# Key transposes and the spread of 1/rms as one group behind the first gate pass of a hybrid decoder layer

## The chip, the cores and the metric

The kernel runs on one core of a Trainium2 chip. The metric is the time on the device in microseconds (us). Its engines are called PE (TensorE; PEld is its weight load), DVE (VectorE), ACT (ScalarE), POOL (GpSimd) and SP (SyncE, which here issues the loads). Each engine works through its own row of instructions in order; where one needs the result of another engine, it waits for a semaphore, and everything behind it on that engine waits with it.

## What is computed

One decoder layer on 256 tokens of width 2048, all in float32. The part around the change is the input projection and what is made of its keys:

```python
h = rmsnorm(x, norm_mix_pre[l])
proj = h @ w_in[l]
xr, yr, q, k, v, g_rnn, g_attn = jnp.split(proj, IN_OFFSETS, axis=-1)
...
q = rope(q.reshape(B, S, N_Q_HEADS, HEAD_DIM), positions)
k = rope(k.reshape(B, S, N_KV_HEADS, HEAD_DIM), positions)
v = v.reshape(B, S, N_KV_HEADS, HEAD_DIM)
y_att = sliding_window_sink_attention(q, k, v, attn_sinks[l])
mix = jax.nn.sigmoid(g_rnn) * (y_rnn @ w_rnn_proj[l]) + jax.nn.sigmoid(g_attn) * (y_att @ w_attn_proj[l])
x = x + rmsnorm(mix @ w_out[l], norm_mix_post[l])
h = rmsnorm(x, norm_mlp_pre[l])
u = jnp.square(jax.nn.relu(h @ w_mlp_up[l]))
x = x + rmsnorm(u @ w_mlp_down[l], norm_mlp_post[l])
```

There are 32 query heads and 4 key and value heads of width 64. `rmsnorm` scales each token by 1/rms; `rope` rotates pairs of columns by angles that depend on the token's position.

## The kernel before

**Products in two parts.** A float32 weight is split into a high part (rounded, `whi`, made by ACT, L117) and a low part (the rest, `wlo`, made by DVE, L123). The transposed activations `hT` are split alike, and a product is three matmuls: high by high, low by high, high by low.

**Weights in half chunks.** `Stream` (from L64) brings the weights in half chunks of 128 x 1024 values, 512 KB each, numbered in the order of use. Raw ones land in four `wraw` buffers (more at the start), high and low parts live in six buffers each (`WHALF`). Before a half chunk is used, `ahead` (L149) sees to it that the parts of six half chunks are written down and that loads run four further. The high part of half chunk n needs the buffer of n - 6, which PE gives back when it is done with that one. A load needs a raw buffer, which DVE's low part gives back.

**Order of work.** After the normalisation and the keys' and values' product (half chunks 0 to 7, banks `kv0` and `kv1`, one for each block of 128 tokens) come four pairs of passes by `b_pass512` (L324): the gate `ga0` (half chunks 8 to 15), the queries `q0` (16 to 23), then `ga1`, `q1` and so on. A half chunk is twelve matmuls of 512 columns. These matmuls and the transposes are pinned in PE's row in the order in which the program is written (`fix`, `ordered`); the rows of ACT and DVE are set by the scheduler, which places instructions by its own rules.

**Side work.** Attention is a generator in the list `waiting`. `pump` (L257) advances it to its next `yield`. In the gate and query passes it is called after each half chunk (`often=True`). The generator begins with `keys_values` (L619). For each block it has ACT scale the values out of the bank, lets DVE rotate the keys (`rope`, L600, which needs sine and cosine of the angles, L567 to L586, times 1/rms of the token) into `k2`, yields, has PE transpose the four groups of `k2` into a bank `pk` and ACT copy them to `kT`, and yields again. At its end `spread_r` (L592) has DVE make two diagonal tiles `dg`, PE multiply them by ones into the bank `pr`, and ACT copy this to `r_all`: 1/rms of every token in every row.

So with one `pump` for each half chunk the first block's rotation is written behind half chunk 8, its transposes behind 9, the second block's transposes behind 11, and the spread behind 12. `kT` is first read by the scores of attention in `ga1`, `r_all` by the recurrent branch (L825) after all eight passes. The banks `pk` and `pr` come from a pool of four, `psm`, which also holds `kv0` and `kv1`; `k2`, the rotation's tiles `ra` and `rb`, and `dg` come from eight rooms `t2`.

## Time and profile before

| | us |
|---|---|
| time, median of 3 runs (1512.39 to 1516.35) | 1514.12 |
| time of the profiled execution | 1514.38 |
| its span, from the first to the last instruction | 1512.6 |
| PE busy | 1490.0 |
| DVE busy | 1126.3 |
| ACT busy | 808.9 |
| HBM traffic, mean over the span | 195 GB/s |

Times in the trace are microseconds from the start of the span. In rows of instructions the first number is the start, the second the length, then follow engine, line, operation and tiles (buffer numbers left out). Matmuls overlap, so the step from one start to the next says what one costs. In a row of waits stand the total, how many, and the longest. The granted clock of PE is given as a share of its full speed.

### The profile page before, as it was taken

Reading aid. Unit: us, or ns where it says so; the run is one execution under the profiler, and the core shown is the slowest. Engines: PE = TensorE matmul, PEld = TensorE weight load, DVE = VectorE, ACT = ScalarE, POOL = GpSimd, SP = SyncE. Lnnn points to the kernel's source line nnn. Section 1 sums busy time; section 2 is a strip of 40 time slices with the busy share of each in tenths; the row PEclk is TensorE's granted clock in tenths of the full one; section 3 lists DMA queues with packets and bytes.
Section 4 is the critical chain, followed back from the end, with each engine's and each line's share of the span. In section 5 each row is a group of like instructions: output and inputs, shape, how many; then the busy total and the mean of one; then the engine's idle time right before and its main releaser. Section 6 shows DMA issues by size and latency. Waiting matters only on the chain.

```text
span 1512.6 us, 19987 instructions
## 1 busy us (share of the span) xinstructions
PE 1490.0 (99%) x7586; PEld 1259.5 (83%) x7586; DVE 1126.3 (74%) x1417; ACT 808.9 (53%) x1110; POOL 1.7 (0%) x9
## 2 busy tenths in 40 slices
PE   9899999999999999999999999999999999999997
PEld 7688778878888888888889888888887888888886
DVE  7557668857758877545667876689987766789898
ACT  6436545747556767444446545455554544555453
POOL 0000000000000000000000000000000000000000
PEclk9899999999999999999999999999999999999999
DMA  7454445365655565656755665655666656578573
GB/s 288 143 189 162 139 157 180 124 202 161 215 177 181 168 224 186 216 191 213 270 192 169 205 208 182 193 195 197 223 216 223 201 180 202 175 252 277 167 252 137
DMA packets 83184, 296.19 MB, mean 196 GB/s; under 512 B 9745, under 2 KB 10001, under 8 KB 82577
## 3 DMA queue, kind: packets, MB, share of 16 engines
q1 hardware_dynamic: 80064, 289.67, 58.3%
q10 hardware_dynamic: 3024, 5.25, 0.9%
q8 instruction: 59, 0.97, 0.3%
q14 instruction: 37, 0.30, 0.1%
HBM read 288.60 MB, written 6.29 MB: 195 GB/s over the span
## 4 chain that ended last, share of the span: by engine, by line
PE 85%; DVE 9%; DMA 4%; ACT 1%; issue 1%; DVEq 0%; SPq 0%; ACTq 0%
PE ps L200 25%; PE ga L200 6%; PE ps L282 6%; PE q L200 6%; DMA wraw<-in_w_dn 4%; PE dQ L200 4%; DVE wlo L123 3%; DVE t L61 3%; PE ps L290 3%; PE s L200 3%; PE dP L200 2%; PE pa L314 2%; PE gr L318 2%; PE pa L318 2%; PE pr L318 2%; PE gr L316 2%
## 5 line engine op out<-in xcount | busy, mean ns | idle before, releaser
L123 DVE TENSOR_TENSOR wlo<-wraw,whi 128x1024 fp32r<-128x1024 f32 x520 | 621.2, 1220 | 242.3 <-ACT whi L117 215.3
L117 ACT CAST whi<-wraw 128x1024 fp32r<-128x1024 f32 x520 | 531.8, 1050 | 432.5 <-DVE wraw L61 77.3
L200 PE MATMUL ps<-h2T,whi 128*128 128x512 f32 x976 | 227.1, 390 | 0.0
L200 PEld LDWEIGHTS ps<-h2T,whi 128*128 128x128 f32 x976 | 181.3, 188 | 36.4
L200 PEld LDWEIGHTS ps<-h2T,wlo 128*128 128x128 f32 x1024 | 127.0, 192 | 2.4
L200 PE MATMUL ps<-h2T,wlo 128*128 128x256 f32 x1024 | 127.9, 283 | 0.0
L200 PE MATMUL dQ<-whi,uT 128*128 128x512 f32 x256 | 95.0, 390 | 0.6 <-ACT whi L117 0.6
L282 PE MATMUL ps<-hT,whi 128*128 128x512 f32 x384 | 89.3, 390 | 0.0
L200 PE MATMUL ga<-whi,hT 128*128 128x512 f32 x256 | 83.7, 400 | 0.0
L282 PEld LDWEIGHTS ps<-hT,whi 128*128 128x128 f32 x384 | 71.3, 188 | 14.3
L200 PE MATMUL q<-whi,hT 128*128 128x512 f32 x256 | 80.3, 391 | 0.0
L303 ACT COPY u<-ps 128x512 f32<-128x512 f32 x32 | 18.7, 586 | 99.6 <-PE ps L200 99.6
L200 PEld LDWEIGHTS ga<-whi,hT 128*128 128x128 f32 x256 | 49.2, 192 | 11.2 <-issue 1.0
L200 PEld LDWEIGHTS dQ<-whi,uT 128*128 128x128 f32 x256 | 48.1, 188 | 10.8 <-ACT whi L117 1.0
L200 PEld LDWEIGHTS q<-whi,hT 128*128 128x128 f32 x256 | 48.1, 188 | 9.9
L61 DVE TENSOR_TENSOR tlo<-t,thi 128x1536 fp32r<-128x1536 f32 x32 | 56.0, 1751 | 0.2 <-ACT thi L140 0.2
L200 PE MATMUL dQ<-wlo,uT 128*128 128x512 f32 x128 | 50.2, 392 | 0.9 <-DVE wlo L123 0.9
L200 PE MATMUL ga<-wlo,hT 128*128 128x512 f32 x128 | 50.8, 397 | 0.0
L314 PE MATMUL gr<-whi,hT 128*128 128x512 f32 x128 | 50.0, 391 | 0.0
L314 PE MATMUL pr<-whi,yrnn 128*128 128x512 f32 x128 | 50.0, 391 | 0.0
L316 PE MATMUL pr<-wlo,yrnn 128*128 128x512 f32 x128 | 49.9, 390 | 0.0
L314 PE MATMUL pa<-whi,yatt 128*128 128x512 f32 x128 | 49.9, 391 | 0.0
(286 smaller groups left out, 2609.3 us busy)
## 6 DMA issues: line engine op xcount, KB each, us to landing
wraw<-in_w_dn SPq DMA_DIRECT2D x128, 512.0 KB, 5.0
wraw<-in_w_up SPq DMA_DIRECT2D x124, 512.0 KB, 4.9
wraw<-in_w_g SPq DMA_DIRECT2D x64, 512.0 KB, 4.8
wraw<-in_w_xy SPq DMA_DIRECT2D x64, 512.0 KB, 4.6
wraw<-in_w_q SPq DMA_DIRECT2D x32, 512.0 KB, 4.3
wraw<-in_w_ap SPq DMA_DIRECT2D x32, 512.0 KB, 4.8
wraw<-in_w_rp SPq DMA_DIRECT2D x32, 512.0 KB, 4.5
wraw<-in_w_out SPq DMA_DIRECT2D x32, 512.0 KB, 4.6
```

The lines of the kernel that those rows point to most:

```text
L61: return lambda *args, **kw: self.pin(method(*args, **kw))
L117: self.pin(self.nc.scalar.copy(hi, src))
L123: self.last_low = self.pin(self.nc.vector.tensor_tensor(lo, src, hi.bitcast(F32), ALU.subtract))
L200: return fix(mm(*args, **kw))
L282: mm(ps[:, f].rearrange("p a b -> p (a b)"), hi[:, k * P : k * P + P], acts[kt // 4][:, kt % 4].rearrange("p a b -> p (a b)"), start=kt == ...
L290: mm(ps[:, f, 1, :], lo[:, k * P : k * P + P], acts[kt // 4][:, kt % 4, 0, :], start=False, stop=kt == KT - 1)
L303: ws.pin(nc.scalar.copy(out, ps[:, :, 1, :]))
L314: mm(banks[tb][n], a[:, 0, t], hi[:, n * 512 : n * 512 + 512], start=first, stop=False)
L316: mm(banks[tb][n], a[:, 0, t], lo[:, n * 512 : n * 512 + 512], start=False, stop=False)
L318: mm(banks[tb][n], a[:, 1, t], hi[:, n * 512 : n * 512 + 512], start=False, stop=last)
```

## The change

`keys_values` no longer yields between a block's rotation and its transposes. It writes both blocks' rotations at the first `pump`, yields eight times, and then writes the transposes of both blocks and the spread together:

```diff
     def keys_values(banks):
+        keys = []
         for tb in range(TB):
             nc.scalar.activation(v_sb[:, tb, :], banks[tb][:, 256:512], AF.Copy, scale=r0[tb])
-            k2 = t2("k2")
-            k4 = k2.rearrange("p (g c d) -> p g c d", g=NKV, c=2)
+            keys.append(t2("k2"))
+            k4 = keys[tb].rearrange("p (g c d) -> p g c d", g=NKV, c=2)
             rope(banks[tb][:, 0:256], tb, NKV, [k4[:, :, 0, :], k4[:, :, 1, :]])
+        for i in range(8):
             yield
+        for tb in range(TB):
             ps = bank(psm, "pk")
             for g in range(NKV):
-                fix(nc.tensor.transpose(ps[:, g * P : g * P + P], k2[:, g * P : g * P + P], ident))
+                fix(nc.tensor.transpose(ps[:, g * P : g * P + P], keys[tb][:, g * P : g * P + P], ident))
             nc.scalar.copy(kT[:, :, tb * P : tb * P + P], ps.rearrange("p (g t) -> p g t", g=NKV))
-            yield
         spread_r()
```

The first place is PE's row at the end of half chunk 9 in the pass `ga0`; the number behind `whi` and `wlo` is the half chunk, the one behind the underscore a buffer's name, `-` is before:

```order
 L200 MATMUL ga0_451<-wlo9_358,hT0_121 128x512
 L200 MATMUL ga0_451<-whi9_356,hT0_121 128x512
-L628 MATMUL pk_498<-ident_111,k2_471 128x128 x4
 L200 MATMUL ga0_451<-whi10_360,hT1_122 128x512
 L200 MATMUL ga0_451<-wlo10_362,hT1_122 128x512
```

The four transposes of the first block are gone from between half chunks 9 and 10; those of the second block, between 11 and 12, and the spread, between 12 and 13, are gone in the same way.

The second place is PE's row where half chunk 16, the first of the pass `q0`, gives way to 17. Before:

```order
L200 MATMUL q0_638<-wlo16_534,hT0_121 128x512
L200 MATMUL q0_638<-whi16_532,hT0_121 128x512
L200 MATMUL q0_638<-whi17_556,hT0_121 128x512
L200 MATMUL q0_638<-wlo17_558,hT0_121 128x512
L200 MATMUL q0_638<-whi17_556,hT0_121 128x512 x2
```

And with the change:

```order
L200 MATMUL q0_618<-whi16_526,hT0_121 128x512
L631 MATMUL pk_637<-ident_111,k2_471 128x128 x4
L631 MATMUL pk_643<-ident_111,k2_481 128x128 x4
L200 MATMUL pr_649<-dg_650,ones_80 128x128
L200 MATMUL pr_649<-dg_653,ones_80 128x128
L200 MATMUL q0_618<-whi17_544,hT0_121 128x512
```

All eight transposes and both matmuls of the spread stand here now, in the same number as before.

The third place is DVE's row from the second block's rotation on, where the low parts of the half chunks 16 and later have moved. Before:

```order
L610 TENSOR_TENSOR rb_525<-kv1_120,ss_433 128x256
L612 TENSOR_TENSOR k2_523<-ra_524,rb_525 128x4x32
L613 TENSOR_TENSOR k2_523<-ra_524,rb_525 128x4x32
...
L596 TENSOR_SCALAR dg_575<-ident_111,st_112 128x128
L596 TENSOR_SCALAR dg_578<-ident_111,st_112 128x128
L123 TENSOR_TENSOR wlo16_534<-wraw16_376,whi16_532 128x1024
L123 TENSOR_TENSOR wlo17_558<-wraw17_456,whi17_556 128x1024
L123 TENSOR_TENSOR wlo18_584<-wraw18_484,whi18_582 128x1024
L123 TENSOR_TENSOR wlo19_602<-wraw19_508,whi19_600 128x1024
```

And with the change:

```order
L610 TENSOR_TENSOR rb_483<-kv1_120,ss_433 128x256
L123 TENSOR_TENSOR wlo18_564<-wraw18_494,whi18_562 128x1024
L612 TENSOR_TENSOR k2_481<-ra_482,rb_483 128x4x32
L613 TENSOR_TENSOR k2_481<-ra_482,rb_483 128x4x32
...
L123 TENSOR_TENSOR wlo19_582<-wraw19_512,whi19_580 128x1024
L596 TENSOR_SCALAR dg_650<-ident_111,st_112 128x128
L596 TENSOR_SCALAR dg_653<-ident_111,st_112 128x128
L123 TENSOR_TENSOR wlo20_600<-wraw20_530,whi20_598 128x1024
```

The low parts 16 to 19, which stood behind all key work, now stand among it: 16 behind the angles (L573), 17 in the first block's rotation, 18 in the second's, 19 ahead of the diagonal tiles. On ACT the high part 16 moves ahead of the load of the sine's table (L575), and the three copies out of `pk` and `pr` move from beside the high parts 16 to 19 to between 22 and 23. All rows behind these places, and the rows of SP and POOL, read as before.

## The prediction

> **What bounds the kernel now.** I read the page's busy times first, then what TensorE (PE) waited for, then a table of stretches around the one long wait.

> ```profile
> span 1512.6 us, 19987 instructions
> PE 1490.0 (99%) x7586; PEld 1259.5 (83%) x7586; DVE 1126.3 (74%) x1417; ACT 808.9 (53%) x1110; POOL 1.7 (0%) x9
> PE pk L628 <- DVE k L613: 7.4, 1, 7.4
> PE kv L470 <- ACT whi L117: 1.5, 2, 0.9
> PE dQ L200 <- DVE wlo L123: 0.9, 2, 0.8
> 34.00:39.35 5.35, 5.35 (x24) 4.11 (x22) 5.27 (x17) 3.85 (x11) 0.00 (x0) 1.00 0.84 259
> 39.35:46.74 7.39, 0.00 (x0) 0.03 (x1) 6.73 (x33) 3.10 (x5) 0.00 (x0) 0.69 0.59 204
> 46.74:52.35 5.61, 5.61 (x16) 4.55 (x17) 1.81 (x8) 0.59 (x1) 0.00 (x0) 0.50 0.00 0
> 52.35:66.90 14.55, 14.55 (x69) 12.10 (x68) 6.06 (x5) 7.19 (x8) 0.00 (x0) 1.00 0.44 140
> 66.90:89.00 22.10, 22.10 (x99) 18.32 (x98) 9.86 (x9) 9.69 (x11) 0.00 (x0) 1.00 0.60 191
> 89.00:1505.00 1416.00, 1411.62 (x7233) 1194.89 (x7231) 1070.13 (x1305) 761.83 (x1035) 0.00 (x0) 1.00 0.59 195
> ```

> PE is busy for 99% of the span, so PE time is what counts. Its waits (total, times, longest) are headed by a single one: 7.4 us before the first key transpose, for the last step of the keys' rotation on VectorE (DVE). No other wait reaches 2 us. In the stretches (length, then busy PE, PEld, DVE, ACT, POOL, granted clock, DMA share, GB/s) the wait is the second row. The row after it shows a second cost: PE is busy again, but at clock 0.50. From 52.35 on the clock is 1.00, and between 89 and 1505 us PE idles only 1416.00 - 1411.62 = 4.4 us. So what is gained here has almost no slack behind it in which to disappear.

> **What goes.** The PE rows around the wait (start, length as modelled, count), and three pieces of the chain that ended last:

> ```profile
> 33.75 0.39 PE L200 MATMUL ga<-whi,hT 128*128 128x512 f32 x1
> 38.96 0.39 PE L200 MATMUL ga<-whi,hT 128*128 128x512 f32 x1
> 46.74 1.09 PE L628 MATMUL pk<-ident,k 128*128 128x128 f32 x4 [7.39 <-DVE k L613]
> 47.48 0.78 PE L200 MATMUL ga<-whi,hT 128*128 128x512 f32 x1
> 52.32 0.65 PE L200 MATMUL ga<-whi,hT 128*128 128x512 f32 x2
> 55.31 0.60 PE L628 MATMUL pk<-ident,k 128*128 128x128 f32 x4
> 55.67 0.48 PE L200 MATMUL ga<-whi,hT 128*128 128x512 f32 x1
> 67.13 0.39 PE L200 MATMUL q<-whi,hT 128*128 128x512 f32 x1
> 55.48 0.44 PE pk L628 x4
> 58.67 0.45 PE pr L200 x4
> 139.53 13.61 PE ga L200 x60
> ```

> A later gate pass runs 60 matmuls in 13.61 us, 0.2268 us each: the full-speed step. Three terms follow. (1) The wait: the last matmul before it starts at 38.96, its successor was due at 39.19, the transpose starts at 46.74: 7.55 us. (2) The first four transposes take 47.48 - 46.74 = 0.74 us at half clock; the same four later take 55.67 - 55.31 = 0.36: 0.38 us. (3) From 47.48 to 52.32 stand 11 gate matmuls, 4.84 us where 11 x 0.2268 = 2.49 would do: 2.35 us. The sum is **10.28 us**. A check from outside: the gate pass lasts from 33.75 to 67.13, 33.38 us; 96 matmuls need 21.77 and its inserts 0.44 + 0.44 + 0.45 = 1.33; 10.28 remain.

> **What is moved.** The eight transposes and the spread (two matmuls, shown as four passes) go behind the first half chunk of the first query pass. They cost PE the same 1.33 us there, in one piece. The nearest row to such a burst is the first of these, attention's; the next two are the first scores and the first product that needs the spread, the last two the ACT copies (ns, least/median/most):

> ```profile
> 137.78 1.75 PE pt L720 x16
> 108.98 1.96 PE sc L200 x24
> 246.31 14.75 PE ps L200 x80
> L629 ACT COPY kT<-pk x2: 582/584/586, 47.9 to 56.5; 128x512 f32<-128x512 f32 x2
> L598 ACT COPY r_all<-pr x1: 366/366/366, 59.7 to 59.7; 128x256 f32<-128x256 f32 x1
> ```

> That is 0.109 us per transpose, so 12 would be 1.31. Three switches between kinds of matmul become one; a switch costs at most 0.44 - 0.36 = 0.08 us by the rows above, so the burst lies between 0.2 us cheaper and, if its three groups start as slowly as the half-clock one, 3 x 0.38 = 1.1 us dearer. I take no difference, as the attention row is at full clock like the burst. The three ACT copies out of it take 0.58, 0.58 and 0.37 us on an engine that was busy 7.19 of 14.55 us there. Their readers come long after: the scores at 108.98, some 99 with the pass moved up by 10, which is 39 us behind the burst; the spread behind the product that starts at 246.31. If that cover were gone, it would cost the copies' 1.5 us. No DMA moves, and the queues of SP and POOL keep their order.

> **What is late next.** Without the wait PE must find the parts of its weights. These rows carry them (half chunk n has a high part from ACT, a low part from DVE; the pass uses 8 to 15):

> ```profile
> 28.46 5.75 DVE L123 TENSOR_TENSOR wlo<-wraw,whi 128x1024 fp32r<-128x1024 f32 x5
> 36.66 1.21 DVE L123 TENSOR_TENSOR wlo<-wraw,whi 128x1024 fp32r<-128x1024 f32 x1
> 38.08 1.22 DVE L123 TENSOR_TENSOR wlo<-wraw,whi 128x1024 fp32r<-128x1024 f32 x1
> 39.43 1.04 ACT L117 CAST whi<-wraw 128x1024 fp32r<-128x1024 f32 x1 [0.63 <-ACT st L398]
> 40.51 1.22 DVE L123 TENSOR_TENSOR wlo<-wraw,whi 128x1024 fp32r<-128x1024 f32 x1
> 40.87 1.28 ACT L575 ACT_TABLE_LOAD   x1
> 43.20 0.19 DVE L573 TENSOR_SCALAR ang<-ang 128x64 f32<-128x64 f32 x1
> 43.43 0.26 ACT L575 ACTIVATE sn<-ang 128x64 f32<-128x64 f32 x1 [1.28 <-DVE ang L573]
> 47.91 0.28 DVE L613 TENSOR_TENSOR k<-ra,rb 128x128 f32<-128x128 f32 x1
> 48.11 0.47 DVE L596 TENSOR_SCALAR dg<-ident,st 128x128 f32<-128x128 f32 x2
> DMA to landing us min/median/max: 3.6/3.8/5.4
> ```

> Low parts 8 to 12 are done at 34.2, 13 at 37.9, 14 at 39.3, 15 at 41.7, all before or beside the wait. So the whole pass can run without anything new. At 12 x 0.2268 = 2.72 us a half chunk, half 10 starts at 39.2, 13 ends at 50.1, the pass ends at 55.5, half 16 at 58.2: there the burst stands, and half 17 follows at 59.6.

> Half 16's high part needs the buffer of half 10, free at 41.9; with 1.04 of ACT and 1.22 of DVE it can be whole at 44.2 or little later, needed at 55.5. On ACT this cast now stands ahead of the sine's table: 42.9 + 1.28 puts the sine at 44.2 instead of 43.4, and every key step about a microsecond later. On DVE the low parts 16 to 19 now stand among the key steps, 4 x 1.22 = 4.9 us more than before. What releases the last is PE itself: high part 19 takes half 13's buffer at 50.1, is done at 51.1, low 19 at 52.4, and the two diagonal tiles for the spread (0.47) at 52.9, a few tenths more with the hand-overs. The burst needs them at 58.2. The last key step, at 47.9 + 0.3 before, has 0.8 us of the sine and the lows 16 to 18 ahead of it, some 53 as a bound and by its order ahead of low 19. So the **slack is about 5 us**, and it moves with PE, as both ends hang on PE's progress. Bounds of this edit: 0 if it holds, 7.55 if all of it were used up and the old wait came back.

> Loads: in 46.74 to 52.35 the DMA share was 0.00, that is, every raw buffer was full while PE crawled. In 66.90 to 89.00, with PE at full clock, 0.60 of the DMA engines' time keeps up.

> Sum: the profiled execution took 1514.38 us for a span of 1512.6, so 1514.38 - 10.28 = **1504.1**, the span 1502.3. It lies 0.26 above the median of the three runs (1514.12), which would make 1503.8; I put down 1504.0.

> [...] The rows: after 16 transposes of 1.75 us (137.78) the next 60 gate matmuls still take 0.2268 us each, and the clock is 1.00 throughout 89 to 1505 us. [...]

> **Rivals.** *Keys late.* The burst waits w because DVE's stretched key steps end after 58.2. For it: DVE was busy 6.73 of 7.39 us there. Against: 5 us of slack. Price: w, and the half clock too if w is long. The clock row 0.69 over 7.39 us means (0.69 - 0.50)/0.50 x 7.39 = 2.8 us at full clock before it fell, so w under 2.8 gives up to 1506.9 and w of 3 gives 1504.1 + 3 + 2.7 = 1509.8. [...]

> *Half clock behind the burst.* PE does not wait, but the clock falls after the transposes: 0.38 + 2.35 = 2.7 us as in the terms above, 1506.8.

> *Given back.* The gain reappears as idle PE time in later passes, since weights that were fetched ahead in the pause no longer are. Against: full raw buffers before, 4.4 us of idle PE in 1416. Half or more given back: 1509.6 to 1514.

> *No effect.* PE stops at half 10 for another reason: 1514. Against: its parts are done at 34.2.

> *Slower: the loads.* Four raw buffers turn in one landing plus 1.04 + 1.22 us, 5.4 + 2.3 = 7.7 us at the worst landing, against 4 x 2.72 = 10.9 us of PE. Before, the pause hid slow landings at this point. With landings over 8.6 us in the first query pass and the two passes behind it (24 half chunks) PE would wait in each; it decides at 10.3 us, where (12.6 - 10.9)/4 x 24 = 10.2 us eat the gain, and 11.2 us give 1504.1 + 15.6 = 1519.7. Against: the worst landing here is 5.4.

> **How the numbers follow.** Forecast, about 10 us faster: 0.85. Keys late: 0.04. Half clock behind the burst: 0.03. Given back: 0.04. No effect: 0.02. Slower by the loads: 0.02. About 0.3%, 4.5 us, is what a measurement of this kernel can tell from no change. The forecast and the first two rivals are faster by more (0.92), the next two within it (0.06), the last slower (0.02). The three runs lay 1.7 below and 2.2 above their median. Low end: 1503.8 - 1.7 - 0.2 for cheaper switches, rounded to 1501.5; high end: 1504.1 + 2.7 for the half clock or a short wait + 1.1 for a dear burst, 1508.0.

> **What would show it.** Right: no PE wait at the key transposes, granted clock 1.00 from 34 us on, first query matmul near 55.5 instead of 67.1, the burst's 12 passes in about 1.3 us near 58.2, diagonal tiles done near 53, idle PE between 80 and 1495 us still about 4 us, span near 1502. Wrong: a PE wait for DVE at line 631, a clock under 1.00 near 60, or new waits of high parts for DMA that PE feels.

## The result and the profile after

The changed kernel took 1504.21 us in the median of four runs (1503.26 to 1507.11), the kernel before 1513.73 in four (1512.39 to 1516.35): a ratio of 0.9938 with a 95% interval of 0.9918 to 0.9958. The forecast was 1504.0, the range 1501.5 to 1508.0. Over all runs of this study the kernel before took 1514.9 in the median of 46, the changed one 1505.95 in the median of 15, 9.0 us less.

The profiled execution of the changed kernel took 1507.11 us, the longest of the four. Its page begins:

```profile
span 1505.3 us, 19987 instructions
PE 1488.2 (99%) x7586; PEld 1257.6 (84%) x7586; DVE 1126.0 (75%) x1417; ACT 810.2 (54%) x1110; POOL 1.7 (0%) x9
```

What PE waited for (total, times, longest), the three largest:

```profile
PE dQ L200 <- DVE wlo L123: 1.7, 3, 0.8
PE kv L470 <- ACT whi L117: 1.4, 2, 0.8
PE s L200 <- DVE wlo L123: 1.4, 1, 1.4
```

The 7.4 us before the key transposes are gone. The two rows on `dQ` and `s` belong to the down projection, near 1060 and 1140 us, and are larger than before; they are followed up below. The same stretches as before, in the same columns (length, busy PE, PEld, DVE, ACT, POOL, granted clock, DMA share, GB/s):

```profile
39.35:46.74 7.39, 7.39 (x35) 6.11 (x34) 6.81 (x31) 5.17 (x7) 0.00 (x0) 1.00 0.72 238
46.74:52.35 5.61, 5.61 (x26) 4.68 (x25) 5.52 (x14) 2.11 (x2) 0.00 (x0) 1.00 0.54 174
78.80:1497.70 1418.90, 1412.45 (x7233) 1194.50 (x7231) 1070.24 (x1305) 763.18 (x1035) 0.00 (x0) 1.00 0.59 194
```

PE is busy through both, at clock 1.00, and the raw buffers' loads no longer stand still in the second (DMA share 0.54, before 0.00). Over the same 7233 matmuls as before, PE now idles 1418.90 - 1412.45 = 6.4 us, against 4.4. The rows around the group on PE, DVE and ACT, from the timeline:

```profile
33.81 0.39 PE L200 MATMUL ga<-whi,hT 128*128 128x512 f32 x1
42.21 1.05 ACT L117 CAST whi<-wraw 128x1024 fp32r<-128x1024 f32 x1 [1.30 <-issue]
44.58 0.26 ACT L575 ACTIVATE sn<-ang 128x64 f32<-128x64 f32 x1
51.07 0.29 DVE L613 TENSOR_TENSOR k<-ra,rb 128x128 f32<-128x128 f32 x1
52.60 0.48 DVE L596 TENSOR_SCALAR dg<-ident,st 128x128 f32<-128x128 f32 x2
55.57 0.39 PE L200 MATMUL q<-whi,hT 128*128 128x512 f32 x1
58.30 1.04 PE L631 MATMUL pk<-ident,k 128*128 128x128 f32 x8
59.17 0.61 PE L200 MATMUL pr<-dg,ones 128*128 128x128 f32 x4
59.53 0.47 PE L200 MATMUL q<-whi,hT 128*128 128x512 f32 x1
59.85 0.39 PE L200 MATMUL q<-wlo,hT 128*128 128x512 f32 x1
```

The pass runs from 33.81 to 55.57 without a gap. The last key step ends at 51.4 and the diagonal tiles at 53.1; the group begins at 58.30, 5.2 us later. It takes 59.53 - 58.30 = 1.23 us, and the matmul behind it 59.85 - 59.53 = 0.32 in place of 0.23, so 1.32 with that.

To follow the gain through the program, I compared the starts of the same matmul, by its number in PE's row, in two traces. With the changed kernel it starts 10.19 us earlier near 80 us and still 10.18 earlier near 1057; then only 7.87 near 1092 and 7.3 from 1163 to the end. So two questions were open: whether the terms of the gain are right, and whether the down projection gives 2.9 us of it back.

### The profile page after: what moved, and what is told of

Its sections match the earlier page's. It is cut to its first block, busy times and chain, and to the rows that moved or that the text cites. A ratio compares the mean times of both kernels' runs of the same rounds, so it can differ in the third digit from the quotient of the medians.

```text
span 1505.3 us, 19987 instructions
## 1 busy us (share of the span) xinstructions
PE 1488.2 (99%) x7586; PEld 1257.6 (84%) x7586; DVE 1126.0 (75%) x1417; ACT 810.2 (54%) x1110; POOL 1.7 (0%) x9
## 4 chain that ended last, share of the span: by engine, by line
PE 85%; DVE 8%; DMA 5%; ACT 1%; issue 1%; DVEq 0%; SPq 0%; ACTq 0%
PE ps L200 25%; PE ga L200 6%; PE ps L282 6%; PE q L200 6%; DMA wraw<-in_w_dn 4%; PE dQ L200 4%; DVE wlo L123 3%; DVE t L61 3%; PE ps L290 3%; PE s L200 3%; PE dP L200 2%; PE pa L314 2%; PE gr L318 2%; PE pa L318 2%; PE pr L314 2%; PE gr L316 2%
## 5 line engine op out<-in xcount | busy, mean ns | idle before, releaser
L123 DVE TENSOR_TENSOR wlo<-wraw,whi 128x1024 fp32r<-128x1024 f32 x520 | 621.6, 1222 | 234.0 <-ACT whi L117 207.3
L117 ACT CAST whi<-wraw 128x1024 fp32r<-128x1024 f32 x520 | 532.9, 1052 | 427.0 <-DVE wraw L61 84.3
L200 PE MATMUL ps<-h2T,whi 128*128 128x512 f32 x976 | 227.1, 390 | 0.0
L200 PEld LDWEIGHTS ps<-h2T,whi 128*128 128x128 f32 x976 | 181.3, 188 | 36.4
L200 PEld LDWEIGHTS ps<-h2T,wlo 128*128 128x128 f32 x1024 | 127.0, 192 | 2.4
L200 PE MATMUL ps<-h2T,wlo 128*128 128x256 f32 x1024 | 127.9, 283 | 0.0
L200 PE MATMUL dQ<-whi,uT 128*128 128x512 f32 x256 | 95.3, 390 | 0.8 <-ACT whi L117 0.8
L282 PE MATMUL ps<-hT,whi 128*128 128x512 f32 x384 | 89.3, 390 | 0.0
L282 PEld LDWEIGHTS ps<-hT,whi 128*128 128x128 f32 x384 | 71.3, 188 | 14.4
L200 PE MATMUL ga<-whi,hT 128*128 128x512 f32 x256 | 81.3, 392 | 0.0
L200 PE MATMUL q<-whi,hT 128*128 128x512 f32 x256 | 80.6, 391 | 0.0
L200 PEld LDWEIGHTS dQ<-whi,uT 128*128 128x128 f32 x256 | 48.1, 188 | 11.3 <-ACT whi L117 1.6
L200 PEld LDWEIGHTS ga<-whi,hT 128*128 128x128 f32 x256 | 48.1, 188 | 10.8 <-issue 1.0
L200 PEld LDWEIGHTS q<-whi,hT 128*128 128x128 f32 x256 | 48.1, 188 | 9.9
L200 PE MATMUL dQ<-wlo,uT 128*128 128x512 f32 x128 | 50.3, 393 | 1.7 <-DVE wlo L123 1.7
L200 PE MATMUL ga<-wlo,hT 128*128 128x512 f32 x128 | 49.9, 389 | 0.0
```

The lines of the kernel that those rows point to most:

```text
L117: self.pin(self.nc.scalar.copy(hi, src))
L123: self.last_low = self.pin(self.nc.vector.tensor_tensor(lo, src, hi.bitcast(F32), ALU.subtract))
L200: return fix(mm(*args, **kw))
L282: mm(ps[:, f].rearrange("p a b -> p (a b)"), hi[:, k * P : k * P + P], acts[kt // 4][:, kt % 4].rearrange("p a b -> p (a b)"), start=kt == ...
```

## The experiments

"Gain at the keys" below is the shift near 80 us against the first profile of the kernel before, corrected for the start of the gate pass (33.75 there), which moves by up to 0.44 us from execution to execution. So the changed kernel has 10.19 + (33.81 - 33.75) = 10.25.

### The pause filled with matmuls

```diff
             ps = bank(psm, "pk")
+            for i in range(31 if tb == 0 else 0):
+                ordered(ps, hT[0][:, 0, 0, 0:P], flat(hT[0])[:, 0:512], start=True, stop=True)
             for g in range(NKV):
```

> The kernel before, with 31 extra 128x512 matmuls into the bank of the first key transposes, just ahead of them; the transposes overwrite the bank. 31 x 0.2268 = 7.0 us fill the 7.55 us pause. Theory (the half clock comes from PE's idleness): the keys are as late as before, the transposes start at about 46.7 us, but the granted clock stays at 1.00 and terms 2 and 3 (0.38 + 2.35 = 2.7 us) go: 1511.0 us. Rival (the clock falls for another reason at this place, such as the transposes): 0.50 behind 46.7 as before, 1513.7 us.

Measured: 1513.64 us (10 runs; before in the same session 1514.96 in 19), ratio 0.9989 (0.9979 to 0.9998). PE's timeline, and the stretch behind the transposes:

```profile
39.49 7.19 PE L200 MATMUL pk<-hT 128*128 128x512 f32 x31
46.97 0.66 PE L630 MATMUL pk<-ident,k 128*128 128x128 f32 x4 [0.29 <-DVE k L613]
47.38 0.48 PE L200 MATMUL ga<-whi,hT 128*128 128x512 f32 x1
46.97:52.35 5.38, 5.38 (x26) 4.53 (x27) 2.71 (x9) 1.64 (x2) 0.00 (x0) 1.00 0.01 3
```

The keys are as late as before, but the clock stays at 1.00, and the transposes take 0.41 us in place of 0.74. The gain at the keys is 2.35 + 0.30 = 2.65, where terms 2 and 3 promised 2.73. So the half clock here follows from PE's idleness, and the two costs, the pause and the slow clock behind it, are separate. The time fell by 1.3 us, half of that, to 1513.64 where 1511.0 was expected. The interval of the ratio reaches from 0.3 to 3.2 us, so the gain of 2.65 us is within it. Two things found further on can lie behind the difference: the half clock cost 2.73 us in the profile that the terms come from and 1.64 to 2.09 in three others, and later stages scatter.

### The pause filled with transposes

```diff
             ps = bank(psm, "pk")
+            for i in range(64 if tb == 0 else 0):
+                fix(nc.tensor.transpose(ps[:, i % 4 * P : i % 4 * P + P], ones, ident))
             for g in range(NKV):
```

> The kernel before, with 64 extra 128x128 transposes of a tile of ones instead of the matmuls, 64 x 0.109 = 7.0 us at full clock. If transposes count as work for the clock: as the filled pause with matmuls, clock 1.00, 1511.0 us. [...]

Measured: 1514.13 us in one run. PE's timeline and the two stretches:

```profile
39.37 7.15 PE L628 MATMUL pk<-ident,ones 128*128 128x128 f32 x64
46.83 0.66 PE L630 MATMUL pk<-ident,k 128*128 128x128 f32 x4 [0.32 <-DVE k L613]
39.37:46.83 7.46, 7.14 (x65) 6.90 (x63) 6.79 (x34) 3.10 (x5) 0.00 (x0) 1.00 0.61 210
46.83:52.35 5.52, 5.52 (x26) 4.63 (x27) 2.84 (x9) 1.64 (x2) 0.00 (x0) 1.00 0.00 0
```

64 transposes alone, for 7.15 us, keep the clock at 1.00, and the gain at the keys is the same 2.65 (2.48 + 0.17). The time by itself says less: 1511.0 was expected with the clock kept, and the single run took 1514.13, where the kernel before took 1514.96 in the same session. Its trace gives 1.3 us back between 250 and 800 us, of which a wait of 1.0 us at L282 that no other profile shows is a part, and 0.8 behind 1057 us; the clock in the rows decides. For these transposes, 128x128 in float32 and started at full clock, the measurement says that they keep it, and the rival of a half clock behind the group has no ground.

### The group three half chunks earlier

```diff
-        for i in range(8):
+        for i in range(5):
             yield
```

> The changed kernel with 5 yields in place of 8: the group stands behind half chunk 13, which ends at 50.2 us. Theory (slack of some 5 us at half chunk 16, that is, keys ready near 51.4 and the diagonal tiles near 51.9): the first block's transposes start at once, the second block's wait about 0.8 us, the diagonal tiles a few tenths more; about 1.2 us lost, clock 1.00, some 9 us faster than before, 1505.4 us. Rival (DVE follows PE closely, no real slack at 16): waits of 4 us and more and the half clock with them, 1509 us or more.

Measured: 1507.47 us (4 runs), ratio 0.9955 (0.994 to 0.997). PE's timeline and two stretches:

```profile
49.63 0.60 PE L631 MATMUL pk<-ident,k 128*128 128x128 f32 x4
51.01 0.63 PE L631 MATMUL pk<-ident,k 128*128 128x128 f32 x4 [0.78 <-DVE k L613]
51.47 0.61 PE L200 MATMUL pr<-dg,ones 128*128 128x128 f32 x4
48.00:52.00 4.00, 3.22 (x21) 2.65 (x21) 4.00 (x12) 2.06 (x4) 0.00 (x0) 1.00 0.61 188
52.00:56.00 4.00, 4.00 (x19) 3.31 (x19) 0.39 (x1) 1.60 (x4) 0.00 (x0) 1.00 0.59 207
```

The first block's transposes wait for nothing, the second's 0.78 us, as expected, and the clock stays at 1.00 in the two stretches at the end. The gain at the keys is 9.73 - 0.44 = 9.29, 0.96 less than with 8 yields. The time is 7.5 us under the session's 1514.96, where some 9 were expected; the same shortfall shows in the changed kernel's later sessions and is taken up below.

### The group two half chunks earlier

The edit is as above, with `range(6)`.

> The changed kernel with 6 yields: the group stands behind half chunk 14, which ends at 52.9 us. With the keys ready near 51.4 and the diagonal tiles near 52 to 53 (a low part less or more ahead of them), PE waits 0 to 0.3 us: the gain of the changed kernel at 80 us, 10.2 against before, to 0.4 us. If DVE follows PE instead: a wait like that with 5 yields, 0.8 us, or more.

Measured: 1507.3 us in one run. PE's timeline:

```profile
52.77 1.03 PE L631 MATMUL pk<-ident,k 128*128 128x128 f32 x8
53.64 0.61 PE L200 MATMUL pr<-dg,ones 128*128 128x128 f32 x4
```

No wait, and a gain at the keys of 10.28. So two half chunks (5.4 us) are what the place could be moved up without loss. This is the slack of about 5 us that the prediction worked out.

### The group five half chunks earlier

The edit is as above, with `range(3)`.

> The changed kernel with 3 yields: the group stands behind half chunk 11, which ends at 44.7 us. Theory: the first block's keys are ready near 48.8 us, so PE waits about 4 us, the second block's near 50.1 and the diagonal tiles near 50.6: about 5 us lost, and as the idle time is longer than the 2.8 us after which the clock fell before, the half clock with it, 2 to 3 us: 1511 to 1512 us, shift against before 2 to 3 us. Rival (4 us of idleness do not bring the half clock): 1509 us.

Measured: 1513.4 us (10 runs), ratio 0.9991 (0.9982 to 1.0001). PE's timeline, and the stretches of the wait and behind it:

```profile
48.70 1.08 PE L631 MATMUL pk<-ident,k 128*128 128x128 f32 x4 [4.05 <-DVE k L613]
50.30 1.09 PE L631 MATMUL pk<-ident,k 128*128 128x128 f32 x4 [0.51 <-DVE k L613]
44.50:48.70 4.20, 0.15 (x2) 0.03 (x1) 4.04 (x17) 1.27 (x3) 0.00 (x0) 0.99 0.48 157
48.70:55.45 6.75, 6.24 (x21) 5.10 (x21) 1.81 (x8) 1.54 (x3) 0.00 (x0) 0.50 0.29 80
```

The wait is 4.05 + 0.51 us, and the clock falls at its very end (0.99 up to 48.7), then stays at 0.50 for 6.8 us. The gain at the keys is 2.57 - 0.14 = 2.43: most of what the change brings is lost again, by the wait of some 5 us and by the slow clock. The time of 1513.4 is 1.6 under the same session's 1514.96, somewhat less than the 2 to 3 expected.

### Three groups in place of one

```diff
             nc.scalar.copy(kT[:, :, tb * P : tb * P + P], ps.rearrange("p (g t) -> p g t", g=NKV))
+            yield
         spread_r()
```

> The changed kernel with a yield behind each block's transposes: three groups, behind half chunks 16, 17 and 18, in place of one. Theory: position matters, grouping does not; 10.2 us at 80 us, at most 0.2 us less for two more switches. Rival (the group itself saves or costs): a difference of 0.5 us or more.

Measured: 1507.16 us in one run, and a gain at the keys of 10.05 + 0.13 = 10.18. In this profile grouping is worth 0.1 us at most; what counts is the place.

### The changed kernel and the kernel before once more

These have no edit.

> The changed kernel once more, for a second profile and more times. Theory (the gain is made at the keys and kept, and what the first profile lost behind 1057 us, 2.3 + 0.6 us, is a scatter of the down projection's loads from execution to execution): the matmuls from 80 to 1050 us stand 10.2 us earlier than before to 0.5 us (the start's own scatter), the loss behind 1057 us is another size, between 0 and 3.5 us, and the time is 9.5 to 10.5 us under before. Rival (given back: the down projection returns about 2.9 us of the gain in every execution): the same 2.9 us again, and 7 to 8 us under before.

> The kernel before once more, for a second profile. Theory (scatter): its own stretch from 1057 to 1170 us differs from the first profile's by 1 to 3 us, likely longer, as the first shows less idle PE there than five profiles of other variants. Rival (given back): the stretch is the same within 0.5 us, and the loss belongs to the variants. Both: the pause of 7.4 us and the half clock stand as before.

Measured: 1507.02 us for the changed kernel (6 runs; before in the same session 1515.41 in 11), ratio 0.994 (0.9928 to 0.9952). Its gain at the keys was 10.28, its later loss 2.5 near 1092 and 3.7 in all. The time was 8.4 us under the kernel before, between the 9.5 to 10.5 expected of scatter and the 7 to 8 expected of a part given back. The second profile of the kernel before lost 0.2 us there: its waits for `dQ` and `s` were 1.8 us, 1.9 in the first. That was what the rival, a part given back, had expected, since all eight profiles of other variants had waits of 2.4 to 4.7 us. Yet among those was the pause filled with matmuls, which gains little. So the last four runs went to this question.

### Two more of the kernel before, one with a single extra matmul, and the changed kernel a third time

The edit of the third is that of the filled pause with `range(1 if tb == 0 else 0)`; the others have none.

> The kernel before, a third profile. PE's waits in the down projection (tiles dQ and s) summed to 1.9 and 1.8 us in its two profiles, and to 2.4 to 4.6 us in the eight of other variants. Theory (scatter of the loads): this kernel shows 2.5 us or more too, here or in the fourth profile. Rival (the later stage gives back a part of what is gained): again under 2.2 us.

> The kernel before, a fourth profile; as the third: 2.5 us or more by the theory of scatter in at least one of the two, under 2.2 us in both by the rival.

> The kernel before with one extra matmul in the pause (31 before): the pause, the half clock and all later times stand as before, within 0.5 us at 80 us. If the down projection's extra waits come with gained time (rival), its waits for dQ and s are those of the kernel before, under 2.2 us. If they come with any program that differs a little, or by chance, 2.5 us or more.

> The changed kernel, a third profile and more times. 10.0 to 10.3 us at 80 us as in both profiles so far. Theory of scatter: waits for dQ and s anywhere from 1.8 to 4.6 us and a time 9.5 to 10.5 us under before. Rival: 3.9 to 4.6 us again, and 7.5 to 8.5 us under before.

Measured: 1517.08, 1513.37 and 1517.64 us in one run each, and 1505.96 for the changed kernel (5 runs; before 1514.72 in 9), ratio 0.9943 (0.993 to 0.9957). PE's waits in the down projection, in the third profile of the kernel before:

```profile
PE dQ L200 <- ACT whi L117: 1.8, 2, 0.9
PE dQ L200 <- DVE wlo L123: 1.7, 3, 0.8
PE s L200 <- DVE wlo L123: 0.6, 1, 0.6
PE dQ L200 <- DVE t L61: 0.3, 1, 0.3
```

With a single extra matmul:

```profile
PE dQ L200 <- DVE wlo L123: 2.0, 4, 0.8
PE dQ L200 <- ACT whi L117: 1.2, 2, 0.8
PE s L200 <- DVE wlo L123: 0.7, 2, 0.5
PE dQ L200 <- DVE t L61: 0.3, 1, 0.3
```

And in the third profile of the changed kernel:

```profile
PE dQ L200 <- DVE wlo L123: 1.7, 3, 0.8
PE dQ L200 <- ACT whi L117: 0.8, 2, 0.6
PE dQ L200 <- DVE t L61: 0.3, 1, 0.3
```

The sums are 4.4 and 4.2 us without any gained time, and 2.8 with 10.28 us gained at the keys. So waits of this size come without the change too, and the first two profiles of the kernel before happened to be at the low end. The waits stand behind weight parts whose 512 KB loads landed in 3.5 to 6.0 us between 1000 and 1170 us in five profiles (the first two of either kernel and that with 6 yields); that the loads make the scatter is likely but not shown. Nothing is shown to be given back, but a small part is not excluded: the third session's time was 8.8 us under the kernel before, again less than the 9.5 to 10.5 expected of scatter alone. All profiles together, against the first of the kernel before (us; the loss is the shift near 1057 us less that at the end):

| profile | gain at the keys | later loss | waits for dQ and s |
|---|---|---|---|
| before, 1st | 0 | 0 | 1.9 |
| before, 2nd | 1.1 | 0.2 | 1.8 |
| before, 3rd | 0.7 | 3.1 | 4.4 |
| before, 4th | 1.1 | 0.5 | 2.4 |
| one extra matmul | -0.1 | 3.0 | 4.2 |
| pause filled, matmuls | 2.65 | 1.5 | 3.0 |
| pause filled, transposes | 2.65 | 0.8 | 2.4 |
| 3 yields | 2.4 | 3.6 | 4.7 |
| 5 yields | 9.3 | 1.5 | 2.7 |
| 6 yields | 10.3 | 2.9 | 3.9 |
| three groups | 10.2 | 2.8 | 4.1 |
| changed, 1st | 10.25 | 2.9 | 4.2 |
| changed, 2nd | 10.3 | 3.7 | 4.6 |
| changed, 3rd | 10.3 | 1.2 | 2.8 |

The gains of the kernel before over its own first profile, 0.7 to 1.1 us, are the second finding of these runs; they are taken up in the next section.

## Why the prediction came out as it did

**The wait (term 1, 7.55 us): right.** The row of the wait says 7.39 to 7.40 us in all four profiles of the kernel before; counted from when the next gate matmul was due, as the prediction did, it is 7.55 or 7.56 in each. It is absent in all variants with 6 or 8 yields.

**The half clock (terms 2 and 3, 2.73 us): right in kind, large in size.** Filling the pause removed it and nothing else. But its size was read off one execution, and it scatters. The second profile of the kernel before, PE's timeline and two stretches:

```profile
46.44 1.08 PE L628 MATMUL pk<-ident,k 128*128 128x128 f32 x4 [7.39 <-DVE k L613]
47.17 0.78 PE L200 MATMUL ga<-whi,hT 128*128 128x512 f32 x1
50.05 0.39 PE L200 MATMUL ga<-wlo,hT 128*128 128x512 f32 x1
39.00:46.44 7.44, 0.05 (x2) 0.04 (x1) 6.77 (x33) 3.10 (x5) 0.00 (x0) 0.76 0.59 208
46.44:50.05 3.61, 3.61 (x11) 3.05 (x12) 1.80 (x8) 0.59 (x1) 0.00 (x0) 0.54 0.00 0
```

Seven gate matmuls, from 47.17 to 50.05, are slow here, where the first profile had eleven: 2.88 - 7 x 0.2268 = 1.29, with 0.37 for the transposes 1.66 us. The third and fourth profiles give 2.09 and 1.64 in the same way. The mean of the four is 2.0, so the sum should have been about 7.55 + 2.0 = 9.6 in place of 10.28. Terms 2 and 3 are what the prediction mis-sized, by 0.7 us together.

**The move: right.** The parts of all eight half chunks were there, the burst cost 1.32 us at full clock (1.33 forecast), the sine came at 44.58 (44.2 forecast), the diagonal tiles at 53.1 (52.9 and a few tenths), the slack was 5.2 us, and the group could move up by two half chunks and not by three. The gain at the keys was 10.25, 10.28 and 10.28 in three profiles, against 10.28 forecast from the first profile of the kernel before.

**Nothing given back: right in the main, open in the last microsecond.** "Idle PE between 80 and 1495 us still about 4" failed in the first profile, 6.4 us. Waits as long stand in the third profile of the kernel before, so this sign alone does not show a return. The later loss in the table averages 2.5 us over the six profiles that gain more than 9 us and 1.6 over the eight others, and the two groups overlap (1.2 to 3.7 and 0 to 3.6). A return of about 1 us is neither shown nor excluded; the rival as the prediction stated it, half of the gain or more, is excluded by the times.

**The time.** 1504.21 us in the first four runs is 0.2 from the forecast, and that closeness is luck: over 15 runs the median is 1505.95, still within the range. Against 46 runs of the kernel before this is 9.0 us, where the corrected sum says 9.6. The 0.6 between them is less than the runs of either kernel scatter (5.6 us from least to most), and stays open; a small return in the down projection would be of that size. The low end of the range was worked out as 1501.9 and put down as 1501.5. Of the rivals, keys late was seen when I made it happen (5 and 3 yields). The loads did not take PE's time in the query passes: in the first profile of the changed kernel PE was busy for 939.73 of the 940 us from 60 to 1000.

## What to carry to other kernels

An engine that works in a fixed order stops at the first instruction whose input is late, even where independent work stands right behind: here PE stood still for 7.4 us in front of half chunk 10, whose parts had been ready since 34.2 us. Write small work that depends on a slow chain behind as much other work as the chain needs, and check that the parts for that other work are already there. On TensorE, price such a pause with the slow clock behind it (1.6 to 2.7 us behind 7.4 us here, nothing behind 0.78), and take that second price from several executions.

## What the runs showed of the hardware

The half clock lasted 10.2 us in one profile and 6.8 or 6.9 in three others. In the first profile of the kernel before it began at 39.35 + 2.8 = 42.2 us and ended at 52.35, 10.2 us; in its second profile at 39.00 + (0.76 - 0.50)/0.50 x 7.44 = 42.9 and ended at 50.05 - (0.54 - 0.50)/0.50 x 3.61 = 49.8, 6.9 us; with 3 yields it lasted 6.8 us. In the third profile of the kernel before, these stretches show it:

```profile
39.00:46.00 7.00, 0.69 (x4) 0.23 (x2) 6.37 (x29) 3.25 (x6) 0.00 (x0) 0.89 0.69 240
46.00:53.00 7.00, 5.92 (x20) 4.94 (x21) 2.86 (x13) 1.09 (x2) 0.00 (x0) 0.62 0.01 2
```

Worked out in the same way, it began at 44.5 and ended at 51.3, 6.9 us again. What sets its length was not shown.
